# Mixer projections summed in one 256-column half, rotary halves swapped by ScalarE copies, the whole triangular inverse on GpSimd

## The chip, the cores and the metric

The kernel runs on one core of a Trainium2 chip, as one program. The metric is the device time of that core in microseconds (us). Before the change the median of three runs is 2493.53 us (2491.78 to 2494.53).

The core's engines each take their own instructions in order: TensorE (PE: matmuls, with weight loads PEld), VectorE (DVE), ScalarE (ACT), GpSimd (POOL) and SyncE (SP, here the DMA queue for weights). They wait for each other through semaphores only.

## The reference

Two layers, each a token mixer and a gated feed-forward, on a sequence of 256 tokens with 2048 features, in float32. Cut to what the change touches:

```python
p = x @ w_in                       # 4 x 1024 (delta net q, k, v, z), 1024 (attention q), 256 (latent), 1024 (index q), small
# group A, 8 heads: gated delta rule in chunks (here of 128 tokens), per head
a_mat = I + tril(beta * (k k^T) * decay, -1)
sol = solve_triangular(a_mat, rhs)                     # a unit lower triangular system per head and chunk
# group B, 8 heads: sparse attention
k, v = split(rms_norm(c_kv) @ w_ukv)                   # keys and values up from the 256-wide latent
q, k = apply_rope(q), apply_rope(k)                    # rot = concat(-x2, x1);  x * cos + rot * sin
q_idx = apply_rope(q_idx)                              # 16 index heads of 64
index = sum_h w[t, h] * relu(q_idx . k_idx)            # top 64 keys of each query are kept
y = concat(A, B) @ w_out;   x = LN(alpha * x + y)
f = conv_ffn(x);            x = LN(alpha * x + f)
```

## The kernel before, in words

Everything is feature-major: a tile has 128 features in its partitions and the 256 tokens in its columns. A float32 product is made from two parts each of weight and operand, high and low, with three matmuls' worth of columns: weight-high times operand-high, weight-high times operand-low, weight-low times operand-high. The operand `X` (and `H` in the feed-forward) holds its high part in columns 0 to 255 and its low part in columns 256 to 511.

**The stream.** Weights come in chunks of eight 128x128 tiles (512 KB, `load`, queued on SyncE, three buffers `raw`). `convert` (L171, L173) makes the parts of a chunk: ScalarE copies `hi` from `raw`, VectorE subtracts to `lo` (three buffers each). `run` (from L177) walks through the chunks: the matmuls of one, then the conversion of the chunk three further on and the load three beyond that. So a chunk's `lo` is wanted by TensorE about three chunks after VectorE can make it, and a new load has its buffer only when the `lo` of the chunk that lay there is done.

**The sum.** `mm3` (from L210) has two forms. Without `fold`, one 512-column matmul of `hi` puts high x high in columns 0 to 255 and high x low in 256 to 511, and a 256-column matmul of `lo` adds to the second half (L219, L221); `evac` then copies the second half out on ScalarE (L311) and VectorE adds the two (L313). With `fold`, three 256-column matmuls sum everything in columns 0 to 255 (L216). `FOLD = 11` has the bits for z (1), index query (2) and k (8); v (16), attention query (4) and delta-net query (32) are without, as are the latent (`chain_c0`, `chain_latent`) and the key up-projection (`kv_unit`).

**The chains.** Everything else is in generators that `run` steps once after each chunk: a `yield` puts what follows one chunk (2.8 to 2.9 us of matmuls) later in the program. A scheduling layer then fixes the order on each engine at build time. In the mixer the chunks run: k, two z, eight index queries (`chain_iq`), four z, two latent projections, two z, then per head v, q, the up-projection for every second head, and the attention query (`chain_att`).

**The inverse** (`chain_inverse`). The 64 diagonal 32x32 blocks of all heads lie one to a partition. Step j (0 to 30) forms an outer product of 31-j by j+1 elements (`Wd`, L749) and subtracts it from the inverse `X` (`BX`, L751); each step needs the one before. `INV_POOL = 16` puts steps 0 to 15 on GpSimd, the others on VectorE. VectorE then copies a transposed form (L754), both go to DRAM from GpSimd's queue (L757, L758), and SyncE's queue reads them back as block tiles `blk` (L766), with weight loads between. `chain_merge` builds the full inverse from the blocks with matmuls; `chain_v` of each head waits for it.

**The rotary** (`rope`, L930 to L933). Two 64-partition products on VectorE write each half of `rt` from the other half of the input times sine, a third makes the input times cosine, a fourth adds.

Of the kernel before, what the change touches and what calls it, by code (L numbers as in the profile page):

```python
# [11 lines left out]
AF = mybir.ActivationFunctionType  # L12
# [21 lines left out]
INV_POOL = 16  # L34
# [12 lines left out]
FOLD = 11  # L47
# [25 lines left out]
# the tiles of the merges: (row block, (chunk, block, number of blocks))  # L73
# [21 lines left out]
class Trunk:  # L95
# [224 lines left out]
    def rsqrt_steps(self, y, x, n):  # L320
# [3 lines left out]
        # Halley  # L324
# [6 lines left out]
        # Newton  # L331
# [138 lines left out]
    def ln_out(self, l):  # L470
        # the last norm
# [87 lines left out]
    def chain_small(self, l, acc):  # L559
# [11 lines left out]
        # log decay and beta  # L571
# [36 lines left out]
        # cumulative decays  # L608
# [29 lines left out]
        # E[j, i] = exp(gc_i - gc_j) for i >= j  # L638
# [57 lines left out]
    def chain_k(self, l, h, acc):  # L696
        nc = self.nc
        V = nc.vector
        kT = self.kT[h] = yield from self.conv_silu(l, 8 + h, acc, 8 if h >= 3 else 0)
# [20 lines left out]
    def chain_inverse(self, l):  # L720
# [3 lines left out]
        # diagonal 32-blocks to one block a partition  # L724
# [8 lines left out]
        # the second chunk's blocks above the diagonal into the first one's room below it  # L733
# [4 lines left out]
        # norms of k  # L738
# [76 lines left out]
    def chain_z(self, l, h, acc):  # L815
        nc = self.nc
        if FOLD & 1:
# [10 lines left out]
    def chain_v(self, l, h, acc):  # L828
        nc = self.nc
        V = nc.vector  # L830
        vT = yield from self.conv_silu(l, 16 + h, acc, 16)
# [41 lines left out]
    def chain_q(self, l, h, acc):  # L873
        nc = self.nc
        V = nc.vector
        qT = yield from self.conv_silu(l, h, acc, 32)
# [48 lines left out]
    def rope(self, dst, u, cosn, sinn):  # L925
# [474 lines left out]
```

## Time and profile before

| | us |
|---|---|
| median of three runs | 2493.53 |
| span of the profiled execution | 2492.8 |
| TensorE busy | 2441.6 (98%) |
| VectorE busy | 1934.6 (78%) |
| ScalarE busy | 1236.9 (50%) |
| GpSimd busy | 285.5 (11%) |

The page gives no other time of the profiled execution than its span. Layer 0's mixer takes about the first 410 us, then comes its feed-forward; layer 1 begins about 1240 us into the span. A busy matmul is shown with its modelled end, so that busy time hides gaps shorter than a matmul's tail. A row of a timeline is start, length, engine, line, operation, and in brackets the idle time of the engine before it with what ended it.

### The profile page before, as it was taken

To read this page: it belongs to the slowest core of one execution; us is meant where nothing else is said; L and a number is where in the kernel's file an instruction comes from. 1 tells how busy PE (TensorE), PEld (TensorE's weight loads), DVE (VectorE), ACT (ScalarE), POOL (GpSimd) and SP (SyncE) were. 2 spreads that over 40 slices of the span, in tenths; PEclk is the share of its full clock that TensorE was granted. 3 is DMA by queue.
4 is the path that set the end of the run, shared out by engine and by line. 5 is a ranking of instruction groups with operands and counts; after the bars stand their busy time and mean duration, and the time that the engine had idled before them with its cause. 6 is when DMAs were issued, how large, how long until landed. Compare 5 with 4: busy or idle time off the path is not lost.

```text
span 2492.8 us, 40103 instructions
## 1 busy us (share of the span) xinstructions
PE 2441.6 (98%) x15016; PEld 2171.0 (87%) x15016; DVE 1934.6 (78%) x3769; ACT 1236.9 (50%) x2137; POOL 285.5 (11%) x377
## 2 busy tenths in 40 slices
PE   9999999999999999999999999999999999999997
PEld 9997888898888888888899888888888888888886
DVE  7789988798888887555589798887888888875555
ACT  5445666454444444444354456664544444444443
POOL 0133101320000000000233221024100000000001
PEclk9999999999999999999999999999999999999998
DMA  7554445465555555666555644454555555555664
GB/s 243 182 172 135 137 147 159 150 196 186 187 191 188 188 187 188 185 186 188 158 189 160 174 133 130 152 163 150 193 187 190 188 189 186 190 186 182 187 187 133
DMA packets 135778, 436.29 MB, mean 175 GB/s; under 512 B 26624, under 2 KB 26912, under 8 KB 135328
## 3 DMA queue, kind: packets, MB, share of 16 engines
q1 hardware_dynamic: 134272, 429.14, 54.1%
q0 software_dynamic: 1312, 4.61, 0.7%
q8 instruction: 117, 1.92, 0.3%
q14 instruction: 77, 0.63, 0.1%
HBM read 429.61 MB, written 3.69 MB: 174 GB/s over the span
## 4 chain that ended last, share of the span: by engine, by line
PE 82%; DVE 12%; DMA 2%; issue 1%; ACT 1%; POOL 1%; SPq 0%; ACTq 0%; DVEq 0%; POOLq 0%
PE acc L219 46%; PE acc L221 24%; PE acc L216 6%; DVE lo L173 4%; PE acc L241 3%; DVE y L520 1%; DMA raw<-w_in 1%; ACT hi L171 1%; DMA G<-gd 1%; DVE YB L302 1%; POOL BX L751 0%; DVE rt L931 0%; DVE idx L1083 0%; PE pd L1059 0%; DVE idx L1066 0%
## 5 line engine op out<-in xcount | busy, mean ns | idle before, releaser
L219 PE MATMUL acc<-X,hi 128*128 128x512 f32 x4000 | 1418.3, 396 | 0.0
L173 DVE TENSOR_TENSOR lo<-raw,hi 128x1024 fp32r<-128x1024 f32 (+1 forms) x821 | 993.6, 1211 | 430.5 <-ACT hi L171 428.4
L171 ACT ACTIVATE hi<-raw 128x1024 fp32r<-128x1024 f32 (+1 forms) x821 | 853.7, 1040 | 868.9 <-PE acc L219 527.2
L221 PE MATMUL acc<-X,lo 128*128 128x256 f32 x4000 | 1121.7, 280 | 4.3 <-DVE lo L173 4.3
L219 PEld LDWEIGHTS acc<-X,hi 128*128 128x128 f32 x4000 | 751.1, 188 | 173.7
L221 PEld LDWEIGHTS acc<-X,lo 128*128 128x128 f32 x4000 | 751.3, 188 | 7.1 <-DVE lo L173 6.5
L219 PE MATMUL acc<-H,hi 128*128 128x512 f32 x1320 | 466.9, 396 | 0.0
L221 PE MATMUL acc<-H,lo 128*128 128x256 f32 x1320 | 372.2, 282 | 0.0
L219 PEld LDWEIGHTS acc<-H,hi 128*128 128x128 f32 x1320 | 248.0, 188 | 60.2
L216 PE MATMUL acc<-X,hi 128*128 128x256 f32 x1408 | 259.6, 284 | 0.6 <-ACT hi L171 0.6
L221 PEld LDWEIGHTS acc<-H,lo 128*128 128x128 f32 x1320 | 247.9, 188 | 0.1
L216 PEld LDWEIGHTS acc<-X,hi 128*128 128x128 f32 x1408 | 220.1, 190 | 2.1 <-ACT hi L171 0.8
L216 PE MATMUL acc<-X,lo 128*128 128x256 f32 x704 | 200.9, 285 | 9.1 <-DVE lo L173 9.1
L216 PEld LDWEIGHTS acc<-X,lo 128*128 128x128 f32 x704 | 133.4, 189 | 10.4 <-DVE lo L173 10.3
L376 POOL COPY racc<-xT 128x256 f32<-128x256 f32 x4 | 2.1, 527 | 1043.6 <-DVE xT L374 1043.6
L390 POOL TENSOR_TENSOR racc<-racc,xT 128x256 f32<-128x256 f32 x56 | 54.9, 981 | 496.8 <-DVE xT L386 496.7
L1255 ACT ACTIVATE sq<-y 128x256 f32<-128x256 f32 x88 | 36.7, 417 | 138.3 <-DVE y L520 138.2
L313 DVE TENSOR_TENSOR u<-acc,c 128x256 f32<-128x256 f32 x232 | 96.3, 418 | 0.3
L520 DVE SCALAR_TENSOR_TENSOR vT<-u,pv,vT 128x255 f32<-128x255 f32 (+1 forms) x176 | 85.1, 483 | 5.9
L520 DVE SCALAR_TENSOR_TENSOR y<-u,fw,y 128x255 f32<-128x255 f32 (+1 forms) x176 | 84.5, 480 | 2.9
L311 ACT ACTIVATE c<-acc 128x256 f32<-128x256 f32 x232 | 84.0, 366 | 4.6 <-PE acc L221 4.6
L241 PE MATMUL acc<-X,hi 128*128 128x256 f32 x512 | 78.1, 295 | 1.9 <-ACT hi L171 1.6
(324 smaller groups left out, 2136.7 us busy)
## 6 DMA issues: line engine op xcount, KB each, us to landing
raw<-w_up SPq DMA_DIRECT2D x336, 512.0 KB, 3.7
raw<-w_in SPq DMA_DIRECT2D x188, 512.0 KB, 3.7
raw<-w_down SPq DMA_DIRECT2D x160, 512.0 KB, 3.6
raw<-w_out SPq DMA_DIRECT2D x48, 512.0 KB, 3.7
raw<-w_out_g SPq DMA_DIRECT2D x16, 512.0 KB, 3.6
raw<-w_up_g SPq DMA_DIRECT2D x16, 512.0 KB, 4.1
raw<-w_down SPq DMA_DIRECT2D x32, 256.0 KB, 3.5
raw<-w_in_g SPq DMA_DIRECT2D x15, 512.0 KB, 4.6
```

Of the source, the lines that this page charges most:

```text
L171: nc.scalar.activation(u.hi[:, o:e], u.raw[:, o:e], AF.Copy)
L173: self.pin(nc.vector.tensor_tensor(u.lo[:, o:e], u.raw[:, o:e], u.hi[:, o:e].bitcast(F32), op=ALU.subtract))
L216: nc.tensor.matmul(acc[:, 0:256], w[:, j * P:(j + 1) * P], xs[:, o:o + 256], start=first and n == 0, stop=last and n == 2)
L219: nc.tensor.matmul(acc[:, 0:512], hi[:, j * P:(j + 1) * P], xs[:, 0:512], start=first, stop=last, skip_group_check=True)
L221: nc.tensor.matmul(acc[:, 256:512], lo[:, j * P:(j + 1) * P], xs[:, 0:256], start=False, stop=last, skip_group_check=True)
L241: self.nc.tensor.matmul(accs[f][:, 0:256], w[:, j * P:(j + 1) * P], xs(k)[:, o:o + 256], start=k == 0 and n == 0, stop=k == nk - 1 and n == 2)
L302: nc.vector.tensor_scalar(dst, src, scale, None, op0=ALU.mult)
L311: nc.scalar.activation(c, acc[:, 256:512], AF.Copy)
L313: nc.vector.tensor_tensor(u, acc[:, 0:256], c, op=ALU.add)
L390: nc.gpsimd.tensor_tensor(self.racc[:, 0, :], self.racc[:, 0, :], x, op=ALU.add)
L520: nc.vector.scalar_tensor_tensor(y[:, s:256], u[:, 0:256 - s], w[:, nt - 1 - s:nt - s], y[:, s:256], op0=ALU.mult, op1=ALU.add)
L1255: nc.scalar.activation(th, y, AF.Tanh)
```

## The change

- v, q, attention query, latent and key up-projection are summed in one half as the others are; `evac` and its VectorE sum go, and the chains read the accumulator itself (the latent is copied out by ScalarE).
- `rope` becomes a generator: ScalarE copies the two halves swapped, then one product of 128 partitions with a sine table of changed sign, on GpSimd for the attention query and key and on VectorE for the index query, then cosine product and sum on VectorE, for GpSimd's case one step later.
- All 31 steps of the inverse are on GpSimd.

```diff
-INV_POOL = 16
-FOLD = 11
...
-    def conv_silu(self, l, j, acc, bit):
+    def conv_silu(self, l, j, acc, grouped=False):
         nc = self.nc
-        if FOLD & bit:
-            u = acc[:, 0:256]
-        else:
-            u = yield from self.evac(acc, self.m256("u"), bit == 0)
+        u = acc[:, 0:256]
+        if grouped:
+            u = yield from self.evac(acc, self.m256("u"), True)
...
-            eng = nc.gpsimd if j < INV_POOL else V
-            eng.tensor_tensor(w, B[:, j, j + 1:32][:, :, None].to_broadcast([64, n, m]),
+            nc.gpsimd.tensor_tensor(w, B[:, j, j + 1:32][:, :, None].to_broadcast([64, n, m]),
                                X[:, j:j + 1, 0:m].to_broadcast([64, n, m]), op=ALU.mult)
-            eng.tensor_tensor(X[:, j + 1:32, 0:m], X[:, j + 1:32, 0:m], w, op=ALU.subtract)
+            nc.gpsimd.tensor_tensor(X[:, j + 1:32, 0:m], X[:, j + 1:32, 0:m], w, op=ALU.subtract)
...
-    def rope(self, dst, u, cosn, sinn):
+    def rope(self, name, u, cosn, sinn, eng):
         nc = self.nc
         V = nc.vector
         t = self.m256("rt")
-        sn = self.c(sinn)
-        V.tensor_tensor(t[0:64], u[64:128], sn[64:128], op=ALU.mult)
-        V.tensor_tensor(t[64:128], u[0:64], sn[0:64], op=ALU.mult)
+        nc.scalar.activation(t[0:64], u[64:128], AF.Copy)
+        nc.scalar.activation(t[64:128], u[0:64], AF.Copy)
+        yield
+        eng.tensor_tensor(t, t, self.c(sinn), op=ALU.mult)
+        dst = self.m256(name)
         V.tensor_tensor(dst, u, self.c(cosn), op=ALU.mult)
+        if eng is not V:
+            yield
         V.tensor_tensor(dst, dst, t, op=ALU.add)
+        return dst
...
-        c = self.t256("c", 4)
-        nc.scalar.activation(c, acc[:, 256:512], AF.Copy)
-        V.tensor_tensor(self.cu[1], acc[:, 0:256], c, op=ALU.add)
+        nc.scalar.activation(self.cu[1], acc[:, 0:256], AF.Copy)
...
-                    self.mm3(acc, hi, lo, 2 * i + k, self.cl[k], k == 0, k == 1)
+                    self.mm3(acc, hi, lo, 2 * i + k, self.cl[k], k == 0, k == 1, True)
...
-        u = yield from self.evac(acc, self.m256("u"))
-        yield
-        ak = self.ak[h] = self.m256("ak")
-        self.rope(ak, u, "cos", "sin")
+        self.ak[h] = yield from self.rope("ak", acc[:, 0:256], "cos", "sin", nc.gpsimd)
...
-        self.rope(q, u, "icos", "isin")
+        q = yield from self.rope("iq", acc[:, 0:256], "icos", "isin", V)
...
-        if FOLD & 4:
-            u = acc[:, 0:256]
-        else:
-            u = yield from self.evac(acc, self.m256("u"))
-            yield
-        q = self.m256("iq")
-        self.rope(q, u, "cos", "sin")
+        q = yield from self.rope("iq", acc[:, 0:256], "cos", "sin", nc.gpsimd)
...
-            self.single(a["w_in"][l][f], xs, KT, done, fold=bool(FOLD & fold))
+            self.single(a["w_in"][l][f], xs, KT, done, fold=True)
```

Three places of the built order follow. The line numbers of the changed kernel are a little lower; names are as above, `idx` is the index sum, `zs` the z gate, `cu` the latent, `d_` the copies in DRAM.

VectorE in layer 0, around the copy of the inverse, before:

```order
L749 TENSOR_TENSOR Wd<-BX 64x60
L1066 SCALAR_TENSOR_TENSOR idx<-rl,widx,idx 128x128
L751 TENSOR_TENSOR BX<-BX,Wd 64x2x30
L1066 SCALAR_TENSOR_TENSOR idx<-rl,widx,idx 128x128
L749 TENSOR_TENSOR Wd<-BX 64x31
L826 SCALAR_TENSOR_TENSOR zs<-th,acc 128x256
L751 TENSOR_TENSOR BX<-BX,Wd 64x31
L826 SCALAR_TENSOR_TENSOR zs<-th,acc 128x256
L754 COPY BX<-BX 64x1024
L173 TENSOR_TENSOR lo<-raw,hi 128x1024
L939 TENSOR_TENSOR cu_2225<-acc,c 128x256
```

Here 51 `lo` stand ahead of the copy in VectorE's list. The same place in the changed kernel:

```order
L818 SCALAR_TENSOR_TENSOR zs<-th,acc 128x256
L171 TENSOR_TENSOR lo<-raw,hi 128x1024 x2
L750 COPY BX<-BX 64x1024
L818 SCALAR_TENSOR_TENSOR zs<-th,acc 128x256
L1050 SCALAR_TENSOR_TENSOR idx<-rl,widx,idx 128x128 x2
L171 TENSOR_TENSOR lo<-raw,hi 128x1024
L1050 SCALAR_TENSOR_TENSOR idx<-rl,widx,idx 128x256 x2
L171 TENSOR_TENSOR lo<-raw,hi 128x1024
```

Now 48 `lo` stand ahead of it, one z gate and four index sums have moved behind it, and no step of the inverse is left on VectorE. In layer 1 the copy stands behind 459 `lo` before and behind 458 now.

SyncE's queue in layer 0, the block loads among the weight loads, before:

```order
L143 DMA raw<-w_in 128x1024 x41
L766 DMA blk<-d_2088 32x8x32 x4
L766 DMA blk<-d_2089 32x8x32 x2
L143 DMA raw<-w_in 128x1024
L766 DMA blk<-d_2089 32x8x32 x2
L143 DMA raw<-w_in 128x1024
```

And in the changed kernel:

```order
L141 DMA raw<-w_in 128x1024 x37
L762 DMA blk<-d_2090 32x8x32 x2
L141 DMA raw<-w_in 128x1024
L762 DMA blk<-d_2090 32x8x32 x2
L141 DMA raw<-w_in 128x1024
L762 DMA blk<-d_2091 32x8x32 x2
```

The first block load stands four weight loads earlier, and more weight loads stand between the block loads.

GpSimd in layer 0, behind the last steps of the inverse, in the changed kernel (`rt` are the rotary products, `qd` the decayed query, E, F and YB the block tiles of the merges); before, this list went from the step of 16x16 straight to the DMAs and had no `rt`:

```order
L745 TENSOR_TENSOR Wd<-BX 64x31
L747 TENSOR_TENSOR BX<-BX,Wd 64x31
L753 DMA d_2090<-BX 64x1024
L754 DMA d_2091<-BX 64x1024
L780 TENSOR_TENSOR E<-blk,cst 128x128 x2
L780 TENSOR_TENSOR F<-blk,cst 128x128 x2
L780 TENSOR_TENSOR YB<-blk,cst 128x128 x2
L780 TENSOR_TENSOR E<-blk,cst 128x128 x2
L780 TENSOR_TENSOR F<-blk,cst 128x128 x2
L780 TENSOR_TENSOR YB<-blk,cst 128x128 x2
L924 TENSOR_TENSOR rt<-rt,cst 128x256 x2
L870 TENSOR_TENSOR qd<-y,eG 128x128
```

The rotary products of the first two keys stand ahead of the first `qd`, behind the merge tiles of the first two heads.

## Rows read from the trace of the kernel before

**Rows 1.** The page's busy line: us, share of span, instructions.

```profile
PE 2441.6 (98%) x15016; PEld 2171.0 (87%) x15016; DVE 1934.6 (78%) x3769; ACT 1236.9 (50%) x2137; POOL 285.5 (11%) x377
```

**Rows 2.** Windows: PE, PEld, DVE, ACT, POOL busy (count), clock, DMA share, GB/s.

```profile
200.00:240.00 40.00, 36.24 (x208) 30.56 (x208) 38.97 (x118) 19.41 (x45) 13.10 (x20) 0.96 0.36 117
240.00:280.00 40.00, 38.31 (x240) 32.81 (x240) 37.84 (x113) 25.23 (x73) 12.60 (x20) 1.00 0.42 135
...
320.00:360.00 40.00, 40.00 (x252) 35.84 (x251) 33.15 (x85) 28.03 (x74) 0.92 (x2) 1.00 0.47 152
...
560.00:600.00 40.00, 40.00 (x230) 34.86 (x230) 33.03 (x54) 19.00 (x29) 0.00 (x0) 1.00 0.58 190
...
1440.00:1480.00 40.00, 37.18 (x225) 32.83 (x224) 38.97 (x121) 19.67 (x48) 11.75 (x18) 0.96 0.37 119
1480.00:1520.00 40.00, 38.41 (x238) 32.53 (x237) 38.24 (x113) 25.45 (x73) 13.73 (x22) 1.00 0.41 133
```

**Rows 3.** Timeline of GpSimd in both inverses: start, length, what, idle before.

```profile
118.28 0.23 POOL L749 TENSOR_TENSOR Wd<-BX 64x31 f32<-64x31 f32 x1 [6.06 <-DMA BX<-d]
...
123.89 0.46 POOL L751 TENSOR_TENSOR BX<-BX,Wd 64x135 f32<-64x135 f32 x1
...
137.17 1.63 POOL L751 TENSOR_TENSOR BX<-BX,Wd 64x247 f32<-64x247 f32 x1
...
142.12 1.61 POOL L749 TENSOR_TENSOR Wd<-BX 64x256 f32<-64x256 f32 x1
143.82 0.80 POOL L751 TENSOR_TENSOR BX<-BX,Wd 64x256 f32<-64x256 f32 x1
...
175.93 0.46 POOL L784 TENSOR_TENSOR E<-blk,cst 128x128 f32<-128x128 f32 x1 [6.55 <-DMA blk<-d]
...
1379.75 0.72 POOL L751 TENSOR_TENSOR BX<-BX,Wd 64x256 f32<-64x256 f32 x1
```

**Rows 4.** Timeline of VectorE in both inverses.

```profile
137.05 1.22 DVE L173 TENSOR_TENSOR lo<-raw,hi 128x1024 fp32r<-128x1024 f32 x1
...
167.44 1.11 DVE L754 COPY BX<-BX 64x1024 f32<-64x1024 f32 x1
...
1373.81 1.65 DVE L173 TENSOR_TENSOR lo<-raw,hi 128x1024 fp32r<-128x1024 f32 x1
...
1380.51 0.42 DVE L749 TENSOR_TENSOR Wd<-BX 64x255 f32<-64x255 f32 x1 [4.23 <-POOL BX L751]
```

**Rows 5.** Timeline of TensorE: second latent chunk, stall of layer 1, second latent chunk.

```profile
160.96 0.28 PE L221 MATMUL acc<-X,lo 128*128 128x256 f32 x1
...
1386.07 0.58 PE L216 MATMUL acc<-X,lo 128*128 128x256 f32 x1 [6.09 <-DVE lo L173]
...
1404.46 0.28 PE L221 MATMUL acc<-X,lo 128*128 128x256 f32 x1
```

**Rows 6.** The chain that ended last: start, us, what, how many instructions.

```profile
1217.96 14.84 PE acc L216 x126
...
1395.49 5.75 PE acc L216 x48
```

**Rows 7.** Groups by line and shape: busy us, mean ns, idle before.

```profile
L313 DVE TENSOR_TENSOR u<-acc,c 128x256 f32<-128x256 f32 x232 | 96.3, 418 | 0.3
...
L930 DVE TENSOR_TENSOR rt<-u,cst 64x256 f32<-64x256 f32 x32 | 14.4, 449 | 0.8
```

**Rows 8.** The inverse's product line, VectorE's part: ns min/median/max, first and last start.

```profile
L749 DVE TENSOR_TENSOR Wd<-BX x30: 174/348/416, 145.7 to 1401.6; 64x255 f32<-64x255 f32 x2, 64x252 f32<-64x252 f32 x2, 64x247 f32<-64x247 f32 x2, 64x240 f32<-64x240 f32 x2
```

**Rows 9.** Windows, the matmuls of L219 alone: PE (count), PEld, clock, DMA.

```profile
200.00:240.00 40.00, 27.86 (x73) 14.38 (x73) 0.96 0.36 117
240.00:280.00 40.00, 25.27 (x68) 12.71 (x68) 1.00 0.42 135
...
320.00:360.00 40.00, 32.89 (x90) 16.77 (x90) 1.00 0.47 152
```

**Rows 10.** A window of 4 us behind the stall of layer 1.

```profile
1388.00:1392.00 4.00, 4.00 (x21) 4.00 (x21) 3.93 (x10) 1.04 (x2) 0.00 (x0) 0.51 0.67 207
```

More of the change, by code (lines that the diff above doesn't have):

```diff
@@ L698, in chain_k @@
         V = nc.vector
-        kT = self.kT[h] = yield from self.conv_silu(l, 8 + h, acc, 8 if h >= 3 else 0)
+        kT = self.kT[h] = yield from self.conv_silu(l, 8 + h, acc, h < 3)
         yield
@@ L816, in chain_z @@
         nc = self.nc
-        if FOLD & 1:
-            u = acc[:, 0:256]
-        else:
-            u = yield from self.evac(acc, self.m256("u"))
-            yield
+        u = acc[:, 0:256]
         th = self.m256("th")
@@ L830, in chain_v @@
         V = nc.vector
-        vT = yield from self.conv_silu(l, 16 + h, acc, 16)
+        vT = yield from self.conv_silu(l, 16 + h, acc)
         kc = self.small("kc", 1)
@@ L875, in chain_q @@
         V = nc.vector
-        qT = yield from self.conv_silu(l, h, acc, 32)
+        qT = yield from self.conv_silu(l, h, acc)
         qd = self.mp.tile([P, P], F32, tag="qd", name="qd", bufs=2)
@@ L1034, in chain_iq @@
         V = nc.vector
-        if FOLD & 2:
-            u = acc[:, 0:256]
-        else:
-            u = yield from self.evac(acc, self.m256("u"))
-            yield
-        q = self.m256("iq")
-        self.rope(q, u, "icos", "isin")
+        q = yield from self.rope("iq", acc[:, 0:256], "icos", "isin", V)
         yield
@@ L1092, in chain_att @@
         sc = 128.0 ** -0.5
-        if FOLD & 4:
-            u = acc[:, 0:256]
-        else:
-            u = yield from self.evac(acc, self.m256("u"))
-            yield
-        q = self.m256("iq")
-        self.rope(q, u, "cos", "sin")
+        q = yield from self.rope("iq", acc[:, 0:256], "cos", "sin", nc.gpsimd)
         yield
@@ L1167, in plan_layer, with nxt @@
         f = 0
-        def nxt(done, fold=0):
+        def nxt(done):
             nonlocal f
-            self.single(a["w_in"][l][f], xs, KT, done, fold=bool(FOLD & fold))
+            self.single(a["w_in"][l][f], xs, KT, done, fold=True)
             f += 1
         for h in range(3, 8):
-            nxt(lambda acc, h=h: (sp(self.chain_k(l, h, acc)), sp(self.chain_inverse(l)) if h == 7 else None), 8)
+            nxt(lambda acc, h=h: (sp(self.chain_k(l, h, acc)), sp(self.chain_inverse(l)) if h == 7 else None))
         for h in range(ZB):
-            nxt(lambda acc, h=h: sp(self.chain_z(l, h, acc)), 1)
+            nxt(lambda acc, h=h: sp(self.chain_z(l, h, acc)))
         for i in range(8):
-            nxt(lambda acc, i=i: sp(self.chain_iq(l, i, acc)), 2)
+            nxt(lambda acc, i=i: sp(self.chain_iq(l, i, acc)))
         for h in range(ZB, ZC):
-            nxt(lambda acc, h=h: sp(self.chain_z(l, h, acc)), 1)
+            nxt(lambda acc, h=h: sp(self.chain_z(l, h, acc)))
         nxt(lambda acc: sp(self.chain_c0(l, acc)))
@@ L1184, in plan_layer @@
         for h in range(ZC, 8):
-            nxt(lambda acc, h=h: sp(self.chain_z(l, h, acc)), 1)
+            nxt(lambda acc, h=h: sp(self.chain_z(l, h, acc)))
         for h in range(8):
-            nxt(lambda acc, h=h: sp(self.chain_v(l, h, acc)), 16)
-            nxt(lambda acc, h=h: sp(self.chain_q(l, h, acc)), 32)
+            nxt(lambda acc, h=h: sp(self.chain_v(l, h, acc)))
+            nxt(lambda acc, h=h: sp(self.chain_q(l, h, acc)))
             if h % 2 == 0:
                 self.kv_unit(l, h // 2)
-            nxt(lambda acc, h=h: sp(self.chain_att(l, h, acc)), 4)
+            nxt(lambda acc, h=h: sp(self.chain_att(l, h, acc)))
         def ln_done(m, acc, last=False):
@@ L1312, in _constants @@
     put("cos", np.concatenate([co, co], 1).T)
-    put("sin", np.concatenate([si, -si], 1).T)
+    put("sin", np.concatenate([-si, si], 1).T)
     co, si = table(64)
     put("icos", np.concatenate([co, co, co, co], 1).T)
-    put("isin", np.concatenate([si, si, -si, -si], 1).T)
+    put("isin", np.concatenate([-si, -si, si, si], 1).T)
     tc = np.concatenate([co, co], 1).reshape(2, P, 64).transpose(1, 0, 2).reshape(P, P)
```

4 lines of the change are left out of this document (1 added, 3 removed).

## The prediction

> **What bounds the kernel now.** The page's busy line comes first [rows 1]: TensorE is busy for 98% of the span, VectorE for 78%, ScalarE for 50%, GpSimd for 11%. So time can only come from two places: from the matmul stream itself, or from the few stretches in which VectorE makes TensorE late. The table of 40 us windows shows where those are [rows 2]. In the feed-forward stage (560 to 600) TensorE runs without a gap, 230 matmuls in 40 us, with VectorE at 33. In the head stage of the mixer (200 to 280, and 1440 to 1520 in layer 1) VectorE is busy for 38 to 39 of 40 us, TensorE is idle for 3.76, 1.69, 2.82 and 1.59 us, and the granted clock is 0.96 in two of them. From 320 on the same work runs at full pace (252 matmuls). The change touches the mixer alone.
>
> The second place is the triangular inverse. In layer 0 GpSimd ends its 16 steps at 144.62 and VectorE takes over without waiting; VectorE's copy of the result stands at 167.44. In layer 1 VectorE is parked behind GpSimd for 4.23 us, until 1380.51, and TensorE, which needs the `lo` halves that VectorE makes, runs dry for 6.09 us, until 1386.07 [rows 3 to 5].
>
> **The change part by part.** Everything is set against the profiled execution, whose span is 2492.8 us; the median of the three runs lies 0.7 above it.
>
> *Mixer sums in one 256-column half.* 26 projections a layer (v, q, attention query, and the two latent ones) with 16 weight tiles each, and 16 tiles of the key up-projection, go from a 512- and a 256-column matmul to three of 256: 432 tiles a layer, 864 in all. A tile costs 40/115 = 0.348 us in the old form (230 matmuls are 115 tiles, [rows 2]). In the new form, which the k and index projections have already, 48 matmuls take 5.75 us, 0.359 a tile; the same form on the feed-forward's operand takes 14.84 us for 126, 0.353 a tile [rows 6]. That is 0.0055 to 0.011 us more, 4.8 to 9.8 us in all, on the engine that sets the end. I take 8, near the row from the mixer itself.
>
> *What VectorE loses.* 34 sums of two halves a layer at 418 ns (14.2 us); of 16 rotaries the two half products, 449 ns for the one and about as much for the other (14.4 us); 8 index rotaries that do one product for two (3.4 us) [rows 7]; and 30 instructions of the inverse at 348 ns (10.4 us) [rows 8]. ScalarE gets two copies a rotary and loses one copy a summed projection; at 50% it has room, and I cost that at nothing. In the head stage 28 us of VectorE's work go, over some 200 us. In its first 80 us that is 11 of 76.8, which leaves 65.6. How much of TensorE's lost time comes back there? Visible idle time in the four windows is 9.9 us, and a granted clock of 0.96 over 40 us costs 1.6, twice [rows 2]: 13.1. By count of tiles it is more: 73 and 68 tiles against 90 in the window from 320 [rows 9]; with the other matmuls (62 and 104 against 72, at about 0.11 us, my estimate from equal neighbours in the row of 252) the two windows lack some 7.0 and 4.2 us, 22 us for both layers. But 65.6 of the remaining 69 us is still 95% of VectorE, so a full recovery is unlikely. I take 13, with 5 and 22 as bounds.
>
> *The whole inverse on GpSimd.* This decides the sign. The listing of the order shows what follows the edit: VectorE's copy of the inverse now stands right behind the 48th `lo` of the kernel, where before it stood behind the 51st (in layer 1 behind the 458th, before the 459th). VectorE takes its instructions in order, so behind that waiting copy are queued two z gates, four index sums, and above all the `lo` halves for all following weight chunks. The 48th belongs to the first chunk of the latent projection; its second chunk, whose `lo` matmuls began at 160.96 and 1404.46, can't start before GpSimd is through [rows 5].
>
> When is that? GpSimd's steps 16 to 30 have the element counts of steps 14 to 0 (an outer product of n by m, then m by n). Steps 0 to 14 took from 118.28 to 142.12, 23.84 us [rows 3]. Six of their instructions are about 0.9 us longer than their neighbours, such as the 1.63 at 137.17, and each of these coincides with a `lo` of VectorE; without them it is 18.4 us. In layer 0 four more `lo` are due until the copy, so GpSimd ends at 144.62 + 18.4 + 3.6 = 166.6. The copy takes 1.1, and the z gate, two index sums and the `lo` ahead of the next matmul about 2.3: TensorE goes on at 170.0 and not at 160.96, **9.0 us later**. In layer 1 the first half ended at 1380.47 with VectorE parked; unparked, it has two `lo` more to meet (1.8), then 18.4 and three `lo` (2.7): 1403.4, and TensorE goes on at 1406.8 against 1404.46, **2.3 us later**. TensorE is ready for that chunk 9 us before or more in layer 0 (it got there at 160.96 without a wait for the inverse), and some 11 us before in layer 1 (1404.46 less the old stall of 6.1 and the slow clock behind it): it stands still. After the stall of 6.09 us in layer 1 the granted clock was 0.51, the lower of its two levels (1.2 GHz and not 2.4), up to about 1392 [rows 10]: 5.9 us at half speed from 1386.07 on, 2.9 us lost. I charge 2.9 for each of the new stalls (1.7 to 3.4). The old stall of layer 1 is inside the 1404.46 already. Together 9.0 + 2.3 + 5.8 = **17.1**, with 8 to 24 as bounds (GpSimd's second half 3 us off either way, the clock).
>
> SyncE's queue moves with it: the block loads that wait for the inverse stand four weight chunks earlier in layer 0, two in layer 1, with weight loads behind them. I cost that at nothing: the weight buffer that the next load wants comes free only with the `lo` behind the copy, so that the load would wait anyway. If that cover is gone, a load of about 4 us stands in the open, once a layer. The merges keep their places among the matmuls and get their blocks about when they did, while TensorE comes later: no wait there.
>
> *Rotary products on GpSimd.* 32 in all, in the head stage. No row shows this product; a GpSimd product of 128x128 takes 0.46 us [rows 3], so I take up to 0.9 for it. It lies off the path as long as VectorE's final addition, one step (2.9 us) behind, finds it done. What it costs VectorE is a rival below.
>
> The Trainium skill bears on it: "SBUF — State Buffer", Who interferes with whom, says that a VectorE instruction with two inputs in SBUF contends with a GpSimd instruction that reads SBUF, and that the later one waits for the whole of the other. The trace agrees for the inverse, by the 1.63 us at 137.17. By that rule the more that runs on GpSimd the dearer each `lo` becomes; the sum with it is the second rival's.
>
> **Sum.** 2492.8 + 8 − 13 + 17.1 = 2504.9, and with the 0.7 to the median **2505 us**: slower by 0.5%.
>
> **The rivals.**
>
> *Faster: GpSimd's second half is cheap.* Its steps have few, long rows (one row of 31 at the end) where the first half had many short ones. If a row costs GpSimd something, the second half is shorter than the first. At 10 us instead of 18.4 it ends at about 157.6 and 1395: layer 0 loses nothing, layer 1 gains 6 and keeps 1.7 for the clock. Then −4 − 13 + 8 = −9, **2485 us**. The sign turns where the two stalls cost 5 us and not 17, that is at a second half of about 12.4 us. Against it: 27 rows of 5 took 0.46 us and four rows of 32 took 0.46 [rows 3], 135 and 128 elements, so that rows seem to cost nothing. Chance 0.13.
>
> *Slower still: the lock takes back the relief.* The `lo` at 1373.81 took 1.65 us, beside GpSimd's work, where the one at 137.05 took 1.22 [rows 4]. If each of the 32 rotary products holds one such VectorE instruction up by 0.4 to 0.8 (that excess, or about the product's own length), VectorE gets 13 to 26 of its 56 us back in a stretch where it is 95% full, and about 5 of the 13 us return: 8 more, **2513 us**. For it speaks that row, and it is what the Trainium skill's rule above would do here. Against it: GpSimd is idle for most of the stage. The same time comes out if the weight loads behind the block loads are late after all. Chance 0.17.
>
> *No change: the relief is whole.* All 22 us come back and the new matmul form costs 4.8: 12 less, **2493 us**. For it: the window from 320, where the same heads run at full pace with VectorE at 33. Against it: the merges and the top-k lie in the first windows and stay on VectorE. Chance 0.15. That the edit doesn't do what it says is no case of its own: the listing has the 256-column matmuls, the GpSimd steps and the copy where I put them.
>
> **How the numbers follow.** Forecast 0.52, at 2505 (2497 to 2513); the rivals 0.13, 0.17, 0.15; 0.03 for times above 2518. Some 0.2%, 5 us, is what a measurement of this kernel can tell from no change: faster means under 2488.5, slower over 2498.5. Faster 0.14; same 0.21 (the third rival and the low edge of the forecast); slower 0.65. The range leaves out about one in ten below and as much above: 2489 to 2518.
>
> **What would show it.** In the profile of the changed kernel: VectorE's copy of the inverse waiting for GpSimd for over 10 us near 152 to 167, and again near 1390 to 1403; GpSimd's steps 16 to 30 in 18 to 23 us; TensorE idle for about 10 us in both places, and the granted clock at half for some us after; in the head stage VectorE at 33 to 36 of 40 us and TensorE with under 1 us idle in a window; 48 matmuls of 256 columns in 5.7 to 5.8 us. The forecast is wrong if GpSimd is through before TensorE needs the second latent chunk, or if the head stage stays as gapped as it is.

## The result and the profile after

The changed kernel takes 2513.95 us (median of four runs, 2513.34 to 2516.72) against 2492.67 (2491.78 to 2494.53): the ratio is 1.0088, 95% interval 1.0075 to 1.0100, so 21 us slower. The forecast was 2505, slower by 12, in a range of 2489 to 2518. The sign and the range held. Of the sum the price of the matmul form came out as put down, the inverse came out within its bounds, the relief of VectorE mostly failed, and a part that was put down at nothing cost up to 7 us.

The busy line of the page after, to be read against [rows 1]:

```profile
PE 2441.8 (97%) x15880; PEld 2212.8 (88%) x15880; DVE 1872.5 (75%) x3561; ACT 1260.0 (50%) x2169; POOL 345.3 (14%) x469
```

VectorE lost 62 us of work, GpSimd gained 60, TensorE's busy time is the same to 0.2 us, and the span is 18.8 us longer (2511.6 against 2492.8). What was added is TensorE's idle time. The inverse first. GpSimd's timeline in layer 0 (start, length, what): step 16 and the last subtraction.

```profile
143.40 0.70 POOL L745 TENSOR_TENSOR Wd<-BX 64x255 f32<-64x255 f32 x1
...
164.73 0.24 POOL L747 TENSOR_TENSOR BX<-BX,Wd 64x31 f32<-64x31 f32 x1
```

VectorE's timeline: the transposing copy in each layer, with the idle time before it in brackets, and in layer 0 the first `lo` behind it.

```profile
165.00 1.02 DVE L750 COPY BX<-BX 64x1024 f32<-64x1024 f32 x1 [10.04 <-POOL BX L747]
...
166.92 1.22 DVE L171 TENSOR_TENSOR lo<-raw,hi 128x1024 fp32r<-128x1024 f32 x1
...
1412.06 1.03 DVE L750 COPY BX<-BX 64x1024 f32<-64x1024 f32 x1 [10.02 <-POOL BX L747]
```

TensorE's timeline at the second latent chunk of each layer, where [rows 5] show it without a wait; then the windows (columns as in [rows 2]) around both inverses and behind the stall of layer 0:

```profile
168.19 0.58 PE L214 MATMUL acc<-X,lo 128*128 128x256 f32 x1 [7.47 <-DVE lo L171]
...
1415.26 0.58 PE L214 MATMUL acc<-X,lo 128*128 128x256 f32 x1 [8.71 <-DVE lo L171]
```

```profile
150.00:190.00 40.00, 32.09 (x248) 31.27 (x247) 22.25 (x38) 15.75 (x26) 16.88 (x31) 0.91 0.64 165
1380.00:1420.00 40.00, 29.05 (x215) 28.15 (x214) 22.47 (x28) 12.50 (x19) 30.22 (x44) 0.88 0.40 121
...
168.00:172.00 4.00, 3.81 (x21) 3.81 (x22) 3.62 (x6) 0.00 (x0) 0.00 (x0) 0.61 0.39 92
```

This is the predicted mechanism, place by place: VectorE parked for 10 us at the copy, the `lo` behind it late, TensorE idle for 7.5 and 8.7 us, and then the lower of the clock's two levels for a few us (a granted clock of 0.61 over 168 to 172, 0.50 over 1416 to 1420). In the kernel before, the same two windows of 40 us have TensorE busy for 38.95 and 33.93.

The head stage, windows after, against [rows 2]:

```profile
200.00:240.00 40.00, 37.01 (x306) 36.08 (x305) 38.98 (x121) 22.12 (x53) 9.96 (x16) 1.00 0.42 137
240.00:280.00 40.00, 36.74 (x297) 35.35 (x296) 30.83 (x97) 25.74 (x71) 16.86 (x29) 1.00 0.35 109
...
1440.00:1480.00 40.00, 37.83 (x313) 37.08 (x312) 35.90 (x98) 21.61 (x46) 11.61 (x20) 1.00 0.46 145
1480.00:1520.00 40.00, 36.43 (x284) 35.22 (x283) 30.13 (x109) 21.61 (x58) 8.10 (x15) 0.96 0.32 106
```

VectorE is relieved in three of the four windows, 30.8 where it had 37.8 and 30.1 where it had 38.2; in the first it is as full as before. TensorE's idle time in the four windows is 12.0 us, where it was 9.9. The relief was there and bought little, 3 us by the runs below. The table of TensorE's waits says for what it waits. Kernel before, 195 to 400 us, then 1440 to 1645 (line, what for: us in total, times, longest):

```profile
PE p L806 <- DVE F L302: 2.1, 1, 2.1
PE acc L221 <- DVE lo L173: 1.9, 4, 0.9
PE p L797 <- ACT us L298: 1.0, 2, 0.5
...
PE acc L221 <- DVE lo L173: 2.4, 2, 2.2
```

And after, 195 to 400:

```profile
PE pw L860 <- ACT us L296: 1.9, 1, 1.9
PE pw L844 <- DVE YB L300: 1.7, 2, 1.3
PE pw L844 <- ACT vp L835: 1.1, 2, 0.6
PE pvt L831 <- ACT av L1016: 0.9, 2, 0.5
...
```

The `lo` waits are gone, but they were only 1.9 and 2.4 us. The rest of TensorE's waits before were mostly for the merges: for tiles F and YB that VectorE makes, and for ScalarE's evictions. After, it waits for these tiles still and more for ScalarE (`us`, `vp`, `av`), 7.9 us in all rows of this view against 6.4 before. The longest wait before, 2.05 us for F in layer 0, is one for VectorE's queue. VectorE's row, then TensorE's:

```profile
206.61 0.81 DVE L302 TENSOR_SCALAR F<-p 32x32 f32<-32x32 f32 x4
```

```profile
207.14 0.46 PE L806 MATMUL p<-F,LT 128*128 128x128 f32 x2 [2.05 <-DVE F L302]
```

The matmuls that F is copied from had ended at 201.09, 5.5 us before. VectorE was busy all that time, with a sum of two halves, a `lo`, three convolution steps, tiles of the other head and a search for the top keys. It takes its instructions in the order of its list, so what it must do ahead of F counts, and not only how much it has to do in all.

To place the 18.8 us I took the first matmul of the same weight chunk in both traces and its start after less its start before. The delay is −1.85 us at 39 us (the first chunks), +8.2 at the start of layer 0's head stage (201), +9.4 at 514, +7.6 at 1374, +13.8 at 1444 (the head stage of layer 1), and +18.8 from 1788 to the end. So 10.0 are lost up to the head stage of layer 0, 6.2 around layer 1's inverse, and 1.2 + 5.0 in the two head stages, these with the dearer matmul form in them; 1.9 and 1.8 are won at the start of the kernel and of layer 1. The first of these gains lies ahead of everything that was changed. The traces of the other runs scatter there from −2.1 to +1.5 us, so a single trace places such delays to some 2 us.

### The profile page after: what moved, and what is told of

It is laid out like the page before. It is cut to its first block, busy times and chain, and to the rows that moved or that the text cites. A ratio compares the mean times of both kernels' runs of the same rounds, so it can differ in the third digit from the quotient of the medians.

```text
span 2511.6 us, 41839 instructions
## 1 busy us (share of the span) xinstructions
PE 2441.8 (97%) x15880; PEld 2212.8 (88%) x15880; DVE 1872.5 (75%) x3561; ACT 1260.0 (50%) x2169; POOL 345.3 (14%) x469
## 3 DMA queue, kind: packets, MB, share of 16 engines
q8 instruction: 124, 2.03, 0.3%
## 4 chain that ended last, share of the span: by engine, by line
PE 80%; DVE 6%; POOL 5%; issue 3%; ACT 3%; DMA 3%; POOLq 0%; ACTq 0%; SPq 0%; DVEq 0%
PE acc L217 41%; PE acc L219 21%; PE acc L214 12%; PE acc L239 2%; DVE lo L171 2%; POOL BX L747 2%; POOL Wd L745 2%; ACT hi L169 1%; DMA raw<-w_in 1%; DMA G<-gd 1%; DMA raw<-w_in_g 1%; DVE y L518 1%; DMA d<-LT 0%; DMA BX<-d 0%; POOL F L780 0%
## 5 line engine op out<-in xcount | busy, mean ns | idle before, releaser
L217 PE MATMUL acc<-X,hi 128*128 128x512 f32 x3168 | 1111.0, 393 | 0.0
L219 PE MATMUL acc<-X,lo 128*128 128x256 f32 x3168 | 884.5, 279 | 0.0
L217 PEld LDWEIGHTS acc<-X,hi 128*128 128x128 f32 x3168 | 593.7, 187 | 141.0
L219 PEld LDWEIGHTS acc<-X,lo 128*128 128x128 f32 x3168 | 593.7, 187 | 0.1
L214 PE MATMUL acc<-X,hi 128*128 128x256 f32 x3072 | 576.2, 286 | 0.1
L214 PEld LDWEIGHTS acc<-X,hi 128*128 128x128 f32 x3072 | 479.6, 190 | 2.5 <-ACT hi L169 0.3
L219 PE MATMUL acc<-H,lo 128*128 128x256 f32 x1320 | 372.2, 282 | 0.0
L219 PEld LDWEIGHTS acc<-H,lo 128*128 128x128 f32 x1320 | 247.9, 188 | 0.1
L239 PE MATMUL acc<-X,hi 128*128 128x256 f32 x512 | 75.4, 288 | 3.0 <-ACT hi L169 2.0
L239 PEld LDWEIGHTS acc<-X,hi 128*128 128x128 f32 x512 | 67.3, 192 | 8.9 <-issue 4.3
L311 DVE TENSOR_TENSOR u<-acc,c 128x256 f32<-128x256 f32 x168 | 70.3, 418 | 0.0
```

The costliest lines, as they stand in the source:

```text
L214: nc.tensor.matmul(acc[:, 0:256], w[:, j * P:(j + 1) * P], xs[:, o:o + 256], start=first and n == 0, stop=last and n == 2)
L217: nc.tensor.matmul(acc[:, 0:512], hi[:, j * P:(j + 1) * P], xs[:, 0:512], start=first, stop=last, skip_group_check=True)
L219: nc.tensor.matmul(acc[:, 256:512], lo[:, j * P:(j + 1) * P], xs[:, 0:256], start=False, stop=last, skip_group_check=True)
L239: self.nc.tensor.matmul(accs[f][:, 0:256], w[:, j * P:(j + 1) * P], xs(k)[:, o:o + 256], start=k == 0 and n == 0, stop=k == nk - 1 and n == 2)
L311: nc.vector.tensor_tensor(u, acc[:, 0:256], c, op=ALU.add)
```

## The experiments

Each experiment was timed beside the kernel before on the same chip. The runs were made on several chips, so the changes are to be compared and not the medians. The change in us is the ratio less 1, times 2490, with its 95% interval; a difference of two changes is uncertain by some 3 to 5 us.

| run | kernel | median, us | change, us |
|---|---|---|---|
| | the changed kernel | 2513.95 | +21.9 (18.7 to 24.9) |
| e2 | before, inverse on GpSimd | 2503.08 | +13.4 (10.0 to 16.7) |
| e1 | changed, inverse split as before | 2504.10 | +12.9 (9.7 to 16.2) |
| e3 | changed, copy on GpSimd | 2521.47 | +31.1 (27.6 to 34.6) |
| e13 | changed, block loads on GpSimd | 2513.88 | +24.2 (20.2 to 27.9) |
| e5 | changed, copy and loads on GpSimd | 2496.83 | +7.0 (4.5 to 9.2) |
| e6 | before, inverse, copy, loads on GpSimd | 2486.12 | −4.5 (−6.7 to −2.5) |
| e7 | before, sums in one half | 2496.59 | +5.7 (3.7 to 8.0) |
| e12 | e6 with sums in one half | 2489.45 | −0.5 (−2.7 to 1.7) |
| e10 | before, second halves unread | 2487.53 | −3.0 (−5.0 to −0.7) |
| e8 | before, up projection in one half | 2519.13 | +27.6 (23.7 to 31.9) |
| e4 | changed, rotary product on VectorE | 2511.48 | +20.4 (16.9 to 23.9) |
| e9 | changed, one more turn ahead of the values | 2510.99 | +20.9 (17.7 to 24.4) |

### The inverse: e2, e1, e3, e13, e5, e6

**e2**: the kernel before with `-INV_POOL = 16` `+INV_POOL = 31`.

> The kernel before with all 31 steps of the inverse on GpSimd and nothing else changed. Theory A: 2508 us, 2503 to 2512, with VectorE's copy waiting some 10 us for GpSimd in both layers. Rival B: 2493 to 2497, no measurable difference to before.

Measured +13.4, at the low edge of theory A. The stall is the predicted one without any of the rest. VectorE's and TensorE's timelines in layer 0:

```profile
160.92 1.02 DVE L754 COPY BX<-BX 64x1024 f32<-64x1024 f32 x1 [8.10 <-POOL BX L751]
```

```profile
164.38 0.58 PE L221 MATMUL acc<-X,lo 128*128 128x256 f32 x1 [7.44 <-DVE lo L173]
```

**e1**: the changed kernel with the later half of the steps back on VectorE.

```diff
+            eng = nc.gpsimd if j < 16 else V
-            nc.gpsimd.tensor_tensor(w, ...)
+            eng.tensor_tensor(w, ...)
```

> The changed kernel with steps 16 to 30 of the inverse back on VectorE, all else as changed. Theory A (the wait of VectorE's copy behind GpSimd costs about 16 us of the 21): 2498 us, 2494 to 2502, and TensorE without a gap of over 2 us ahead of the second latent chunk in layer 0. Rival B (the 256-column form and the head stage cost the time): 2510 to 2514.

Measured +12.9, between the two expectations: neither theory had it right. Taking the inverse back wins 9.0 of the 21.9, but the other two parts cost 12.9. Some of that is again the inverse: VectorE's step 16 now stands behind 451 `lo` in layer 1, where it stood behind 453, and it waits longer for GpSimd than the 4.23 us of [rows 4]. In layer 0, where it didn't wait before, it waits for 3.20 us (at 147.92). VectorE's timeline in e1 in layer 1, then TensorE's, against its 6.09 of [rows 5]:

```profile
1384.47 0.42 DVE L746 TENSOR_TENSOR Wd<-BX 64x255 f32<-64x255 f32 x1 [10.10 <-POOL BX L748]
```

```profile
1386.75 0.58 PE L214 MATMUL acc<-X,lo 128*128 128x256 f32 x1 [8.24 <-DVE lo L171]
```

**e3**: the changed kernel with the waiting copy taken off VectorE.

```diff
-        V.tensor_copy(B, X.rearrange("p i j -> p j i"))
+        nc.gpsimd.tensor_copy(B, X.rearrange("p i j -> p j i"))
```

> The changed kernel with the transposing copy of the inverse on GpSimd too, so that VectorE never waits for the inverse. Theory A says that it is VectorE's queue behind the copy that stops TensorE, not the inverse being late for the merges: 2498 us, 2494 to 2503, no gap ahead of the second latent chunk. Rival C (the merges want the inverse at once, so that the stall only moves down to them): 2508 to 2514, with TensorE idle for some 10 us at the first merges.

Measured +31.1: worse than the changed kernel, and both expectations missed. VectorE no longer waits and the second latent chunk is on time. But TensorE stands still a little later, for the latent's transposes, and for longer:

```profile
186.31 0.90 PE L949 MATMUL ptc<-cst,cu 128*128 128x128 f32 x3 [11.74 <-ACT cu L941]
```

SyncE's own waits, 140 to 200 us, and its queue in e3:

```profile
SPq L762 <- DMA d<-BX: 14.9, 1, 14.9
```

```profile
175.97 1.49 SPq L762 DMA_DIRECT2D blk<-d  x3
```

SyncE is parked for 14.9 us at the first block load, and the weight loads stand behind it; VectorE's next `lo` (182.74) had waited 14.80 us for its `hi`, and that for the load. In the changed kernel SyncE is parked at the same place for 13.2 us; there VectorE's wait at the copy hides it. The prediction had charged this queue nothing as long as VectorE's copy covers it, and some 4 us a layer if the cover is gone. The reasoning held, the price didn't: the load that comes late is not one load's length late but as late as the inverse.

**e13** and **e5**: the block loads moved, without and with the copy.

```diff
-                nc.sync.dma_start(
+                nc.gpsimd.dma_start(
                     self.blk[32 * q:32 * q + 32 * w, n], ...)
```

> The changed kernel with the block loads alone on GpSimd's queue; the transposing copy stays on VectorE. If the copy on VectorE is what holds TensorE first, as predicted (9.0 and 2.3 us of stall and 2.9 of clock a layer), and the loads stand hidden behind it, nothing changes: 2509 to 2514. If the loads alone were the cause, 2495 to 2500.

> The changed kernel with the transposing copy behind the inverse and the block loads of the merges, which stand on SyncE's weight queue, both issued by GpSimd. Theory E: with the copy alone moved, SyncE still waited 14.9 us at its first block load with the weight loads behind it, and that was the whole stall; with the loads off SyncE nothing of TensorE's queue stands behind the inverse any more, both stalls go, and the time is 2494 (2488 to 2500) against the changed kernel's 2513. Theory F: the merges need the blocks so soon that the wait only moves to them (TensorE waits for the merge tiles instead), 2505 to 2515.

e13 +24.2: no gain. With the copy still on VectorE, its wait at the copy is the same 10.04 us. e5 +7.0: 15 us less than the changed kernel and 24 less than e3. So two queues held TensorE, each enough by itself: taking away one wait shows nothing, or worse, and only both together show the price. Windows around the inverses in e5, with TensorE busy for 39.52 and 37.70 us instead of 32.09 and 29.05, at full clock:

```profile
150.00:190.00 40.00, 39.52 (x322) 38.83 (x321) 28.41 (x44) 19.35 (x32) 33.59 (x45) 1.00 0.67 200
1380.00:1420.00 40.00, 37.70 (x305) 36.87 (x304) 29.97 (x45) 17.95 (x29) 33.84 (x45) 1.00 0.61 188
```

The inverse itself is no faster; GpSimd's copy takes longer there, and the first block loads are issued 7 us behind the end of the steps:

```profile
171.46 0.24 POOL L747 TENSOR_TENSOR BX<-BX,Wd 64x31 f32<-64x31 f32 x1
171.76 3.13 POOL L750 COPY BX<-BX 64x1024 f32<-64x1024 f32 x1
...
178.55 2.35 POOL L762 DMA_DIRECT2D blk<-d  x4 [2.59 <-DMA d<-BX]
```

Hardly anyone waits for that: TensorE's wait table from 195 us on has 0.2 us for the merge tiles that GpSimd makes of them.

**e6**: the same three on the kernel before (`INV_POOL = 31`, copy and loads on GpSimd).

> The kernel before with all 31 steps of the inverse, the copy and the block loads on GpSimd; sums and rotary halves as they were. Theory E: the inverse alone cost 11.7 us over the kernel before (2503), all of it through the two queues, so without them it is at or below the kernel before, whose own stall at the second layer's inverse (6 us) goes too: 2484 (2478 to 2490). Theory F: 2495 to 2503.

Measured −4.5 (−6.7 to −2.5): 2486.1 against 2489.9, the fastest kernel of this study and faster than both kernels of the case. The old stall of layer 1 went too:

```profile
150.00:190.00 40.00, 39.51 (x273) 36.51 (x272) 31.59 (x54) 20.59 (x35) 31.95 (x44) 1.00 0.74 216
1380.00:1420.00 40.00, 39.45 (x282) 36.94 (x281) 28.98 (x46) 19.45 (x31) 32.74 (x42) 1.00 0.64 197
```

So moving the whole inverse to GpSimd was not the mistake; leaving its two in-order followers where they were is what cost.

### The head stage: e8, e7, e10, e12, e4, e9

**e8**: the form alone, where nothing waits for VectorE.

```diff
-                            lambda acc, j=j, v=v: sp(self.chain_up(l, j, v, acc)))
+                            lambda acc, j=j, v=v: sp(self.chain_up(l, j, v, acc)), fold=True)
...
-        u = yield from self.evac(acc, self.t256("u", 3), j < 2)
+        u = yield from self.evac(acc, self.t256("u", 3), True)
```

> The kernel before with the up projection of the feed-forward, 1344 tiles a layer, also summed in one 256-column half, and nothing else: the price of the form where nothing waits for VectorE. By the two spacings in the trace of before (0.359 and 0.348 us a tile) 2688 tiles cost 2688 x 0.011 = 30 us, 2521 (2510 to 2525). Rival: the form costs nothing of itself and its evictions are cheaper (one ScalarE copy in place of copy and add), 2485 to 2492.

Measured +27.6. A window of the feed-forward in e8, against the 230 matmuls of [rows 2]:

```profile
560.00:600.00 40.00, 40.00 (x335) 40.00 (x334) 29.59 (x47) 19.33 (x28) 0.00 (x0) 1.00 0.59 184
```

335 matmuls of 256 columns are 111.7 tiles, 0.358 us each, against 0.348: 0.010 more, 27 us for 2688 tiles. The 864 tiles of the change cost 8.7 (8.9 by the measured 27.6); the prediction's 8 holds.

**e7**: the sums alone (all projections folded; rotary and inverse as before).

```diff
-FOLD = 11
+FOLD = 63
...
-            self.single(a["w_in"][l][f], xs, KT, done, fold=bool(FOLD & fold))
+            self.single(a["w_in"][l][f], xs, KT, done, fold=True)
```

> The kernel before with the projections' sums in one half alone (values, queries, attention queries, attention keys, latents); the inverse and the rotary products stay. The prediction's two terms for this, +8 for the form and -13 of relief, would give 2486 (2482 to 2490). What the changed trace shows from the head stages (about +7.7 with the rotary part in it) would give 2496 to 2500: the waits of TensorE for lo went, but waits for the merges and their evictions came in their place.

Measured +5.7, as the trace of the changed kernel had it and not as the prediction's terms would. With 8.7 for the form, 3.0 is left as relief. Here, and in e10, it is the sums alone that VectorE loses, 14.2 us a layer; the rotary halves, about as much again, stay.

**e10**: the relief without the form. The matmuls stay as before; the copy and the addition of the second half are left out, so that this half is missing from the result.

```diff
-FOLD = 11
+FOLD = 63
...
-            self.single(a["w_in"][l][f], xs, KT, done, fold=bool(FOLD & fold))
+            self.single(a["w_in"][l][f], xs, KT, done, fold=bool(11 & fold))
```

> The kernel before with the sums still made over 512 columns, but with only the first half read for values, queries, attention queries, attention keys and latents: the copy of the other half on ScalarE and the addition on VectorE are left out, and with them that half's small share of the result. This is VectorE's relief without the price of the form. The prediction's relief, 13, gives 2477 (2470 to 2485). Theory H, that the relief is small because TensorE's waits go elsewhere: 2485 to 2489 (the 2496.6 of the sums alone less the 8.7 of the form: 2488).

Measured −3.0 (−5.0 to −0.7): the same 3 us, by another way. Its windows:

```profile
200.00:240.00 40.00, 37.25 (x216) 31.44 (x214) 38.80 (x122) 18.70 (x45) 11.66 (x21) 0.96 0.39 125
240.00:280.00 40.00, 37.35 (x234) 32.10 (x234) 34.55 (x106) 23.60 (x67) 11.38 (x19) 1.00 0.38 125
```

VectorE is as full as ever in the first window (38.80), where the merges are, and emptier in the second (34.55 against 37.84), where TensorE's idle time didn't fall (2.65 against 1.69). The waits moved inside VectorE. In both head stages, counted from the same weight chunk, TensorE's waits for VectorE come to 8.5 us before and 9.0 in e10: those for `lo`, 4.3, are gone, and the others rose from 4.2 to 9.0. VectorE's row for the longest of them, 2.03 us for F, with what stands ahead of it:

```profile
202.31 0.43 DVE L930 TENSOR_TENSOR rt<-acc,cst 64x256 f32<-64x256 f32 x1
...
205.40 0.18 DVE L302 TENSOR_SCALAR F<-p 32x32 f32<-32x32 f32 x1
```

The matmuls that F is copied from had ended at 198.63. From 202.31 to 205.40 VectorE makes seven instructions of the first two keys' rotary. Before, these stand behind F (from 212.78 on), since the keys' chain had two turns more for its sum. So e7 and e10 change the order too, and their 3 us are the relief with this order in it; an order that keeps F ahead was not run.

**e12**: e6 with the sums in one half, that is e5 with the old rotary products.

> The kernel before with the sums in one half and the whole inverse, its copy and its block loads on GpSimd: the kernel of the run with copy and loads on GpSimd (2496.8), but with the old rotary products on VectorE. What is between the two is the price of the new rotary part. If the three parts add up, 2496.6 (sums alone) less 3.8 (the inverse in that form) = 2493, the rotary part costing 4; if the rotary part helps, as the relief of VectorE would have it, 2498 to 2502.

Measured −0.5: 2489.45, below both expectations. Against e5 the new rotary part costs 7.5 us (7.2 by e1 less e7). The two tables of TensorE's waits from 195 to 400 us show one part of it. In e5:

```profile
PE pw L860 <- ACT us L296: 1.9, 1, 1.9
PE pw L844 <- DVE YB L300: 1.8, 2, 1.3
PE pw L844 <- ACT vp L835: 1.1, 2, 0.6
PE pvt L831 <- ACT av L1016: 1.1, 2, 0.7
...
```

In e12:

```profile
PE p L806 <- DVE F L302: 1.9, 1, 1.9
PE pl L1101 <- DVE iq L933: 1.0, 3, 0.5
...
```

With the new rotary part TensorE waits for evictions by ScalarE, 4.1 us in these rows, that it doesn't wait for in e12. All waits of a view, both layers, counted from the same weight chunk, come to 8.4 + 9.0 us in e5 and 6.2 + 6.4 in e12: 4.8 more, of the 7.5. Those for ScalarE are 9.4 more, those for VectorE 4.8 less. What ScalarE did ahead of two of these evictions, its timeline in e5:

```profile
202.94 0.38 ACT L922 ACTIVATE rt<-acc 64x256 f32<-64x256 f32 x1
203.34 0.38 ACT L1016 ACTIVATE av<-pva 128x256 f32<-128x256 f32 x1
...
248.49 0.42 ACT L530 ACTIVATE th<-y 128x256 f32<-128x256 f32 x1 [1.50 <-DVE y L518]
248.81 0.26 ACT L296 ACTIVATE us<-p 128x128 f32<-128x128 f32 x1
```

Ahead of `av` stand two of the new copies. Ahead of `us`, the longest wait, stands none: there ScalarE was idle for 1.50 us, since the `th` before it in its list waited for VectorE's `y`.

**e4**: the changed kernel with the attention's rotary products on VectorE (`nc.gpsimd` to `nc.vector` in the two calls).

> The changed kernel with the rotary products of attention query and key on VectorE and not on GpSimd. Rival D (GpSimd's products hold VectorE's two-input instructions up and take the relief back): 2504 to 2509. Theory A: within 4 us of the changed kernel, 2510 to 2518, since VectorE has room in the head stage and TensorE's gaps there wait for the merge chain.

Measured +20.4, no different from the changed kernel within the intervals. The lock between VectorE and GpSimd, the second rival, is not seen to cost time here; e4 takes it away, but also gives VectorE 32 products more. GpSimd's products in the changed kernel (ns min/median/max):

```profile
L924 POOL TENSOR_TENSOR rt<-rt,cst x32: 714/776/984, 211.2 to 1644.8; 128x256 f32<-128x256 f32 x32
```

The longest is 0.2 us over the median, so hardly any of them was held up. The one held up is VectorE: beside these 32 products, 14 of its instructions in the changed kernel's trace take longer than their like, by 6.0 us in all (one of 128x2 took 0.69 us at 320.13, where 0.16 is usual). The rival wanted 13 to 26.

**e9**: the changed kernel with `-YPV = 1` `+YPV = 2`.

> The changed kernel with the turn that lies between a value tile's SiLU and its transposes on TensorE doubled, since without the eviction of the sum the value chain comes one turn earlier than before. Theory G: the relief of the head stages was turned into TensorE's waits for these chains (4.7 us of pw and pvt waits in the first layer's head stage that the kernel before did not have); with the turn given back these waits go and the time falls by 4 to 8 us, 2506 to 2510. Rival H: the waits lie in the merge chains whatever their place, or the VectorE never cost that much in the head stages; 2512 to 2517.

Measured +20.9, no different from the changed kernel; its 2510.99 lies between the two expectations. The waits moved and fell little, 6.1 us in all rows of this view against 7.9. TensorE's waits in e9, 195 to 400 us:

```profile
PE pr L853 <- ACT ptp L1108: 1.6, 1, 1.6
PE p L802 <- DVE F L300: 1.5, 2, 0.9
...
```

The 1.9 us of `pw` for `us` are gone, and `pr` waits for another ScalarE eviction instead. Theory G fell: to move one step does not take the waits away. H is what is left; no run shows it by itself.

## Why the prediction was right in sign and 9 us short

By its own steps. Parts added one at a time, from the table: sums +5.7 (e7), rotary +7.2 (e1 less e7), the whole inverse +9.0 (the changed kernel less e1): 21.9. These shares hold for this order of adding; with the inverse first it is 13.4 (e2), and if the sums keep their 5.7, 2.8 is left for the rotary part.

1. **The form, 8.** Right: 8.7 by e8's price a tile; 48 matmuls take 5.76 us in the chain of the changed kernel too.
2. **The relief, −13 (5 to 22).** Wrong. For the sums, half of the work that VectorE loses in the head stage, it is −3.0 in e10 and in e7; what the other half, the rotary halves, gives back is inside the rotary part, which costs 7.2 all the same. Together the two come to +4.2 where −13 was forecast. The step that failed is "Visible idle time in the four windows is 9.9 us, and a granted clock of 0.96 over 40 us costs 1.6, twice: 13.1". That this idle time was mostly a wait for VectorE is right: 8.5 us of 11.4 in the wait tables of before. What failed is that it would go as VectorE's load goes. Only the waits for `lo`, 1.9 and 2.4 us, went; those for tiles of the merges, which stand in VectorE's list behind other work, rose instead (e10), since the edit also moved the keys' rotary ahead of them. Of what the forecast wanted to see there, VectorE at 33 to 36 of 40 us came in one window (35.9), two were emptier (30.8 and 30.1) and the first stayed full (39.0); TensorE under 1 us idle in a window did not come at all (2.2 to 3.6 us). "If the head stage stays as gapped as it is", its own condition of failure, is what came. Its third rival (relief whole) is refuted.
3. **ScalarE's copies, nothing.** "At 50% it has room, and I cost that at nothing" failed for the rotary part as a whole: it costs 7.2 and 7.5 in two pairs of runs. Why is in part open. The waits that came are for ScalarE's evictions (e5 against e12); before `av` the two copies stand directly ahead, but before the longest, `us`, ScalarE was idle behind a wait for VectorE. The turns that `rope` now takes and its reading of the accumulator were not separated from the copies. Nor do the two pairs lose their time in the same place: e1's trace is 8 us behind e7's at the start of layer 0's head stage already, e5's 3 behind e12's.
4. **The inverse, 17.1 (8 to 24).** The mechanism was right in each place. GpSimd's later half took 21.6 us (143.40 to 164.97), 22.0 forecast; the end 164.97 against 166.6; the stalls 7.5 and 8.7. Forecast and stall in layer 1 differ in place (1412 against 1403), since the stream was 7.6 us late by then. The clock cost less in layer 0 than the 2.9 put down: 0.61 of full speed over the 3.8 us of work in 168 to 172 is 1.5. As a term it was within its bounds and high: 13.4 alone over the kernel before (e2), which is what was forecast; 16.2 by the delays of the changed kernel's own trace; 9.0 when added last (e1), where the split form that it replaces had got worse (8.24 us of stall in layer 1 instead of 6.09; 5.63 in e7, without the rotary part).
5. **SyncE's loads, nothing.** Right as put (e13: no change), and the warning about the cover was right too (e3), but with 12 us a layer (e3 less e5, 24 for two) where it said about 4: it took the length of the load for the length of the wait.
6. **Rotary products on GpSimd, up to 0.9 us each, hidden.** 0.78 each. Not wholly hidden: VectorE's final addition waited for them eight times, 10.6 us in all; e4, without these waits, is 1.5 us less, which is within its uncertainty.
7. **The rivals.** "Faster" is refuted by GpSimd's 21.6 us. "Slower still" gave nearly the right time, 2513, from a cause that the runs do not bear out: e4 wins next to nothing without the lock, and late loads cost nothing as long as the copy waits (e13). "No change" needed the relief.

The Trainium skill's rule that the prediction cited ("SBUF — State Buffer", Who interferes with whom) agrees with the inverse here: beside GpSimd's steps VectorE's `lo` takes up to 1.70 us (at 1386.45) where it takes 1.22 alone. Beside the rotary products its price is the 6.0 us of VectorE's time under e4.

The errors against the forecast sum, in the order of adding above: relief of the sums +10.0, rotary +7.2, form +0.7, inverse −8.1, together +9.8; forecast +12.1, measured +21.9 by the ratio. That the sum stayed in its range is in part luck, errors of opposite sign.

## What to carry to other kernels

Before the relief of an engine is counted as time, read from the wait table which of its instructions are waited for, and from its timeline what stands ahead of them: work that goes shortens a wait only if it stood ahead, and an edit that takes turns out of a chain can put other work there. When a slow step is moved to an idle engine, move with it everything that waits for its result in an in-order queue (here the copy on VectorE and the loads on SyncE), and test them together, since two waits that overlap hide each other. A busy share of 50% does not say that there is room: what is added can stand ahead of something that the bounding engine waits for, as the copies do ahead of `av`.

## What the runs showed of the hardware

The contention of GpSimd and VectorE showed itself almost whole in two pairs of instructions. GpSimd's copy took 2.06 us in e3's layer 1 and 3.13 in e5's layer 0, where a `lo` of VectorE (171.74, 1.22 us) had begun 0.02 us earlier: 1.07 longer, nearly the whole `lo`. In e6 the order was the other way. The two rows, GpSimd's and VectorE's:

```profile
168.01 2.06 POOL L754 COPY BX<-BX 64x1024 f32<-64x1024 f32 x1
```

```profile
168.73 2.42 DVE L173 TENSOR_TENSOR lo<-raw,hi 128x1024 fp32r<-128x1024 f32 x1 [1.58 <-ACT hi L171]
```

The copy ends at 170.07, and the `lo` takes its usual 1.1 to 1.2 us from there. So the later of the two waits for the end of the other, which is what the Trainium skill says in the section named above.

Three matmuls of 256 columns cost 0.010 us more a tile than one of 512 and one of 256, though the columns are the same 768. In e8 the weight loads fill the window (PEld 40.00 of 40, against 34.86), so the third weight load a tile is the likely cause; no run separates it.

The lower clock, too, was a part of each long stall's price: where the changed kernel has a granted clock of 0.91 and 0.88 around the inverses, e5 and e6, without the stalls, have 1.00.
